# Residual products of the second block as 512 columns, an up projection one quarter ahead, and PSUM banks as fixed places

## The chip, the core and the metric

The kernel runs on one core of one Trainium2 chip, as one launch. The time is the device time of that launch in microseconds. Before the change it is 3416.86 us, the median of three runs (3407.37 to 3424.01). The profile is one further execution.

## What is computed

512 tokens of width 1024 go through two blocks of two layers each. Block 1 (norm, a mixed attention and convolution stage, an output product) is left as it is. The change is in block 2, of which each of the two layers computes:

```python
xn = rmsnorm(x, norm1_g[l])
h = xn @ w_in[l]                      # four mixers: gdn, diff, swa, mlstm
...
branch = jnp.einsum('bsnw,nwd->bsnd', ys, w_branch[l])
gate = jax.nn.sigmoid(jnp.einsum('bsd,dne->bsne', xn, w_gate[l]))
x = x + jnp.sum(gate * branch, axis=2) @ w_out[l]          # 1024 x 1024
xn = rmsnorm(x, norm2_g[l])
x = x + jnp.square(jax.nn.relu(xn @ w_mlp1[l])) @ w_mlp2[l]  # 1024 -> 4096 -> 1024
```

After the last layer a final norm is written out. All products must hold float32 accuracy.

## The kernel before

Every large product is made of three: activations and weights are each split into a high and a low part (fp32r), and high x high, high x low and low x high are summed in a PSUM bank of 128 x 512 floats. `terms(kt)` (L111) lists the 3 x kt products of a tile: first, for each k, the high weight with both activation parts, then the low weights. A token tile j is 128 of the 512 tokens.

**Weights.** `weights` (L346 on) takes 2048 columns' worth of weight per partition (8 k tiles of 256 columns, or 4 of 512), in two halves. Each half is loaded from memory by SP into `w` or `wx` (L295), copied to the high part on ACT (L367, 128 x 1024), and subtracted on POOL in four pieces of 256 columns to give the low part (L371). High and low parts have two buffers each, so a chunk can be prepared once the chunk before the last is through on PE.

**Products.** `gemm_T` (L397 on) has the weights stationary and 512 tokens moving (L405); `gemm_tile` (L408 on) has a token tile's activations stationary and weight columns moving (L413). Both open a bank with the tag `g`.

**Second block, layer by layer.** First the mixers: two chains of work, `gdn` and `others`, run side by side, the latter on banks with the tag `bS`, rope transposes and attention scores among them; `gdn` uses halves of the two `A` banks. Then gates and branches (`branch`), which sum into `mix`; `gated` splits `mix` into high and low on ACT (L1034) and DVE (L1035), chunk by chunk of 128 channels. Then w_out: `add_last` multiplies in four column blocks of 256, adds each tile to the residual x on DVE (L1012), does blocks 0 and 1 for all tiles, then blocks 2 and 3 tile by tile, each tile followed by its norm: squares on ACT (L322), a power on POOL (L301), a scaling on DVE (L329), eight transposes on PE (L334) into two banks, and the split into high and low (L337, L338).

Then the MLP in four quarters c of the 4096 hidden values. `up(c, e)` makes 256 of them: relu on ACT (L1055), square on POOL (L1056), high part on ACT (L1057), low part on DVE (L1058), into buffers `fhi` and `flo`, two of each. The down projection of a quarter is 4 column blocks x 4 tiles x 24 products, with the add L1012. The order is up(0), up(1, 0), down(0), up(1, 1 to 3), up(2, 0), down(1), and so on; the last is up(3, 1 to 3), then down(3) through `add_last` with the next layer's norm, or the final one.

**What sets the order.** The code is recorded in the order in which it is written; a scheduler then orders each engine's queue by that order and by its own idea of when operands are there. Engines run their queues in order. PSUM tiles came from pools: block 1 had two banks for each of `g`, `S`, `T`, `O`; block 2 two for `g`, three for `bS`, one for `bO` and two for `A`. Each use of a bank was a new tile, which the pool put into whichever bank of its tag was free. The pool of block 1 was closed before that of block 2 was opened.

Of the kernel before, what the change touches and what calls it, by code (L numbers as in the profile page):

```python
# [10 lines left out]
FT = mybir.dt.float32  # L11
# [7 lines left out]
T, D, L = 512, 1024, 2  # L19
NT = T // 128  # L20

PSUM_BUFS = {"g": 2, "S": 2, "T": 2, "O": 2, "bS": 3, "bO": 1}


class Arena:
# [22 lines left out]
A, AR, B0, B, C0, CR, C = Arena(), Arena(FR), Arena(), Arena(), Arena(), Arena(FR), Arena()  # L48
# [16 lines left out]
M1, M2, MR = Arena(), Arena(), Arena(FR)  # L65
# [22 lines left out]
X, G0, G, GR, P, PR = Arena(), Arena(), Arena(), Arena(FR), Arena(), Arena(FR)  # L88
# [17 lines left out]
def seg(w_ap, lo, n, kt=8):  # L106

    return w_ap[:, lo:lo + n].rearrange("(k p) n -> p k n", p=128)


def terms(kt):  # L111


    return [(0, y, k) for k in range(kt) for y in range(2)] + [(1, 0, k) for k in range(kt)]


class Consts:
# [5 lines left out]
    def add(self, name, a):  # L123
        a = np.asarray(a, np.float32)
        full = np.zeros((128, a.shape[1]), np.float32)
        full[:a.shape[0]] = a
        self.off[name] = (self.n, a.shape[1])
        self.n += a.shape[1]
        self.cols.append(full)
# [63 lines left out]
class K:  # L193
# [67 lines left out]
    def t(self, shape, tag):  # L261
        ar, tile_, turn = next(a for a in reversed(self.arenas) if tag in a[0].at)
        at, n, bufs = ar.at[tag]
        i = turn[tag] = (turn.get(tag, -1) + 1) % bufs
        m = math.prod(shape[1:])
        assert m <= n, tag
        t = tile_[:shape[0], at + i * n:at + i * n + m]
        if len(shape) == 2:
            return t
        d = " ".join("abcd"[:len(shape) - 1])  # L270
        return t.rearrange("p (%s) -> p %s" % (d, d), **{"abcd"[i]: shape[i + 1] for i in range(len(shape) - 1)})
# [2 lines left out]
        return self.t([128, n], tag)  # L274

    def bank(self, tag):
        return self.ps.tile([128, 512], FT, name="ps_" + tag, tag=tag, bufs=PSUM_BUFS[tag])

    def small_dma(self, dst, src):
        with self.nc.allow_non_contiguous_dma("small"):  # L280
# [701 lines left out]
class Block2:  # L982
# [23 lines left out]
        self.diff_lambda()  # L1006
        run((self.gdn(), 360), (self.others(box), 315))

    def add(self, n):

        x, cols = self.k.x, slice(n * 256, (n + 1) * 256)
        return lambda acc, j: self.nc.vector.tensor_add(x[:, j, cols], x[:, j, cols], acc[:, :256])  # L1012

    def add_last(self, segs, a, tiles):

        k = self.k
        for n in range(2):
            k.gemm_M(k.weights([segs[n]], 8), a, 8, 256, self.add(n))
        ws = [k.weights([segs[n]], 8) for n in (2, 3)]
        for j in range(NT):  # L1020
            for n in (2, 3):
                k.gemm_tile(ws[n - 2], a, 8, 256, j, self.add(n))
            for t in tiles:
                t(j)

    def gated(self):

        k, nc, l, ins = self.k, self.nc, self.l, self.ins
        mix = k.t([128, 8, T], "mx")
        for n in ORDER:  # L1030
            self.branch(n, mix)
        mhi, mlo = k.t([128, 8, T], "ahi"), k.t([128, 8, T], "alo")
        for c in range(8):
            nc.scalar.activation(mhi[:, c], mix[:, c], AF.Copy, scale=0.5)  # L1034
            nc.vector.scalar_tensor_tensor(mlo[:, c], mix[:, c], 0.5, mhi[:, c].bitcast(FT), op0=OP.mult, op1=OP.subtract)  # L1035
        xnT, tile_ = k.norm(ins["norm2_g_2"][l])
        self.add_last([seg(ins["w_out_2"][l], n * 256, 256) for n in range(4)], (mhi, mlo), [tile_])
        return xnT

    def mlp(self, xnT, norms):  # L1040
        k, nc, l, ins = self.k, self.nc, self.l, self.ins
        w1, w2 = ins["w_mlp1_2"][l], ins["w_mlp2_2"][l]
        hs = {}

        def up(c, e):

            if e == 0:
                hs[c] = k.t([128, 8, T], "fhi"), k.t([128, 8, T], "flo")
            w = k.weights([seg(w1, c * 1024 + e * 256, 256)], 8)
            for b in range(2):  # L1050
                def ev(acc):
                    hh, hl = hs[c]
                    m = 2 * e + b
                    r, s = k.slot("fr"), k.slot("fs")
                    nc.scalar.activation(r, acc, AF.Relu)  # L1055
                    nc.gpsimd.tensor_mul(s, r, r)  # L1056
                    nc.scalar.activation(hh[:, m], s, AF.Copy)  # L1057
                    nc.vector.tensor_sub(hl[:, m], s, hh[:, m].bitcast(FT))  # L1058
                k.gemm_T(w, xnT, 8, b * 128, ev, pieces=2 if c == e == 0 else 1)
        for c in range(4):  # L1060
            for e in range(1 if c else 0, 4):
                up(c, e)
            segs = [seg(w2[c * 1024:(c + 1) * 1024], n * 256, 256) for n in range(4)]
            if c < 3:
                up(c + 1, 0)
                for n in range(4):
                    k.gemm_M(k.weights([segs[n]], 8), hs[c], 8, 256, self.add(n))
            else:
                res, tiles = norms()
                self.add_last(segs, hs[c], tiles)  # L1070
        return res

    def others(self, d0):
# [730 lines left out]
def body(tc, ins, const_ap, cmap, out):  # L1804
    nc = tc.nc
    with ExitStack() as ctx:
        k = K(tc, ins, const_ap, cmap, ctx)
        psum = lambda n: tc.tile_pool(name="ps%d" % n, bufs=2, space=bass.MemoryType.PSUM)
        by_tile = lambda a: a.rearrange("(j p) d -> p j d", p=128)
        x_in = by_tile(ins["x"][0])  # L1810

        def to_layer(g_ap):

            res, tile_ = k.norm(g_ap)
            return res, [tile_, k.spill]

        def last():
            _, tile_ = k.norm(ins["final_norm_g_2"], out=k.x)
            return None, [tile_, lambda j: nc.sync.dma_start(by_tile(out)[:, j], k.x[:, j])]

        def between():
            _, tile_ = k.norm(ins["final_g"], out=k.x)
            res, tiles = to_layer(ins["norm1_g_2"][0])
            return res, [tile_] + tiles

        k.tp = "T"
        with k.open("A", A, AR), psum(1) as k.ps:
            blocks = [Block1(k, l) for l in range(L)]
            with k.open("C", C0, CR, C):
                x = k.x = k.t([128, NT, D], "x")  # L1830
                hT, tile_ = k.norm(ins["norm_g"][0])
                for j in range(NT):
                    k.load(x[:, j], x_in[:, j])
                    if j == 0:
                        k.load_ident()
                    if j == 1:
                        blocks[0].load_first()
                    tile_(j)
                k.load_consts()
            for l in range(L):  # L1840
                hT = blocks[l].layer(hT, None if l else x_in,
                                        (lambda: to_layer(ins["norm_g"][l + 1])) if l < L - 1 else between)
        k.tp = "bS"
        with psum(2) as k.ps:
            banks = [k.ps.tile([128, 512], FT, name="ps_A%d" % i, tag="A%d" % i, bufs=1) for i in range(2)]
            k.halves, k.turn = [b[:, z:z + 256] for z in (0, 256) for b in banks], 0
            for l in range(L):
                b = Block2(k, l)
                with k.open("M", M1, M2, MR):
                    b.mixers(hT)  # L1850
                with k.open("X", X):
                    with k.open("G", G0, G, GR):
                        xnT = b.gated()
                    with k.open("P", P, PR):
                        hT = b.mlp(xnT, (lambda: to_layer(ins["norm1_g_2"][l + 1])) if l < L - 1 else last)


# [24 lines left out]
```

## Time and profile before

| | us |
|---|---|
| median of three runs | 3416.86 |
| the profiled execution | 3411.11 |
| its span, first to last instruction | 3409.2 |
| PE busy (share of the span) | 3200.6 (94%) |
| DVE busy | 1568.6 (46%) |
| ACT busy | 1401.8 (41%) |
| POOL busy | 1400.4 (41%) |
| mean granted clock of PE | 0.987 |

The stages of the profiled execution, read from its order of time: block 1 to about 794 us; first layer of block 2: mixers to 1412, gates and branches to 1666, w_out to 1726, MLP to 2106; second layer: mixers to 2720, gates to 2973, w_out to 3034, MLP and final norm to the end. A granted clock of 1.00 is 2.4 GHz, 0.50 is 1.2 GHz. Ends of matmuls in the trace are modelled, so distances between starts say more than durations; "idle before" is the time that the engine stood still ahead of a row, with what ended it.

### The profile page before, as it was taken

Reading aid. Unit: us, or ns where it says so; the run is one execution under the profiler, and the core shown is the slowest. Engines: PE = TensorE matmul, PEld = TensorE weight load, DVE = VectorE, ACT = ScalarE, POOL = GpSimd, SP = SyncE. Lnnn points to the kernel's source line nnn. Section 1 sums busy time; section 2 is a strip of 40 time slices with the busy share of each in tenths; the row PEclk is TensorE's granted clock in tenths of the full one; section 3 lists DMA queues with packets and bytes.
Section 4 is the critical chain, followed back from the end, with each engine's and each line's share of the span. In section 5 each row is a group of like instructions: output and inputs, shape, how many; then the busy total and the mean of one; then the engine's idle time right before and its main releaser. Section 6 shows DMA issues by size and latency. Waiting matters only on the chain. (4 is left out here: it accounts for less than half of the span.)

```text
span 3409.2 us, 52506 instructions
## 1 busy us (share of the span) xinstructions
PE 3200.6 (94%) x19358; PEld 2693.2 (79%) x19358; DVE 1568.6 (46%) x3832; ACT 1401.8 (41%) x3129; POOL 1400.4 (41%) x1809
## 2 busy tenths in 40 slices
PE   7899989997899899999999999999989999999998
PEld 6576667666788778788889888788778788789998
DVE  5746584664687565322321114577675412321112
ACT  3245423543465465523332222455565532332222
POOL 5332352314411322455566554421332355555554
PEclk9999999998999999999999999999999999999999
DMA  5341324213211211433323333221121243323231
GB/s 136 91 107 44 65 78 118 63 40 89 67 30 32 73 57 38 137 112 118 99 87 93 93 99 86 72 49 32 51 68 50 87 132 110 112 80 99 87 100 68
DMA packets 334449, 277.13 MB, mean 81 GB/s; under 512 B 114024, under 2 KB 312040, under 8 KB 332784
## 3 DMA queue, kind: packets, MB, share of 16 engines
q1 hardware_dynamic: 334048, 273.38, 27.3%
q8 instruction: 152, 2.49, 0.3%
q14 instruction: 105, 0.86, 0.1%
q0 software_dynamic: 144, 0.39, 0.1%
HBM read 257.26 MB, written 16.86 MB: 80 GB/s over the span
## 5 line engine op out<-in xcount | busy, mean ns | idle before, releaser
L405 PE MATMUL ps_g<-all 128*128 128x512 f32 (+1 forms) x5184 | 1255.9, 394 | 21.0 <-DVE B L723 12.0
L405 PEld LDWEIGHTS ps_g<-all 128*128 128x128 f32 x5184 | 951.1, 190 | 209.8 <-DVE B L723 13.7
L371 POOL TENSOR_TENSOR all<-all,all 128x256 fp32r<-128x256 f32 x1024 | 784.4, 799 | 616.0 <-PE ps_g L405 197.1
L413 PE MATMUL ps_g<-all 128*128 128x256 f32 (+1 forms) x4224 | 658.6, 303 | 10.2 <-ACT all L305 2.9
L413 PEld LDWEIGHTS ps_g<-all 128*128 128x128 f32 x4224 | 565.5, 194 | 45.2 <-issue 12.3
L371 POOL TENSOR_TENSOR all<-X,all 128x256 fp32r<-128x256 f32 x448 | 328.2, 765 | 486.3 <-ACT all L367 379.7
L413 PE MATMUL ps_g<-all,P 128*128 128x256 f32 x3072 | 377.1, 285 | 15.1 <-ACT P L1057 7.8
L413 PEld LDWEIGHTS ps_g<-all,P 128*128 128x128 f32 x3072 | 374.2, 194 | 17.3 <-DVE X L1012 8.5
L367 ACT ACTIVATE all<-all 128x1024 fp32r<-128x1024 f32 x256 | 268.4, 1055 | 123.7 <-PE ps_g L405 61.0
L367 ACT ACTIVATE all<-X 128x1024 fp32r<-128x1024 f32 x112 | 118.2, 1055 | 384.1 <-PE ps_g L413 239.6
L371 POOL TENSOR_TENSOR all<-A,all 128x256 fp32r<-128x256 f32 x144 | 135.6, 973 | 305.4 <-ACT all L367 212.3
L1012 DVE TENSOR_TENSOR X<-X,ps_g 128x256 f32<-128x256 f32 x160 | 66.8, 420 | 321.3 <-PE ps_g L413 321.3
L301 POOL TENSOR_TENSOR M<-M,ct 128x2 f32<-128x2 f32 (+1 forms) x64 | 52.0, 814 | 382.2 <-DVE M L300 362.2
L1058 DVE TENSOR_TENSOR P<-P,P 128x512 fp32r<-128x512 f32 x64 | 44.3, 692 | 346.8 <-ACT P L1057 346.8
L405 PE MATMUL ps_g<-G,all 128*128 128x512 f32 x768 | 176.0, 389 | 0.4 <-DVE G L1799 0.4
L405 PEld LDWEIGHTS ps_g<-G,all 128*128 128x128 f32 x768 | 144.0, 188 | 31.1 <-DVE G L1799 1.2
L492 ACT ACTIVATE A<-A 128x128 f32<-128x128 f32 (+3 forms) x160 | 89.2, 558 | 101.0 <-DVE A L490 100.0
L1799 DVE SCALAR_TENSOR_TENSOR G<-G,ps_g 128x512 f32<-128x512 f32 x48 | 32.9, 685 | 212.3 <-PE ps_g L405 212.3
L1057 ACT ACTIVATE P<-P 128x512 fp32r<-128x512 f32 x64 | 40.4, 632 | 182.6 <-POOL P L1056 182.6
L457 PE MATMUL ps_bS<-ct,M 128*128 128x128 f32 x456 | 76.4, 283 | 37.4 <-DVE M L1678 9.0
L1301 ACT COPY M<-ps_A 128x256 f32<-128x256 f32 x224 | 81.3, 376 | 73.2 <-PE ps_A L1300 62.4
L1387 PE MATMUL ps_A<-M 128*128 128x128 f32 x640 | 101.8, 286 | 2.6 <-ACT M L1381 1.7
(379 smaller groups left out, 4265.8 us busy)
## 6 DMA issues: line engine op xcount, KB each, us to landing
all<-in_w_in_dram SPq DMA_DIRECT2D x100, 512.0 KB, 3.7
X<-in_w_mlp_dram SPq DMA_DIRECT2D x64, 512.0 KB, 3.6
all<-in_w_mlp_dram SPq DMA_DIRECT2D x64, 512.0 KB, 3.6
all<-in_w_gate_dram SPq DMA_DIRECT2D x40, 512.0 KB, 3.7
X<-in_w_gate_dram SPq DMA_DIRECT2D x24, 512.0 KB, 3.6
A<-in_w_in_dram SPq DMA_DIRECT2D x16, 512.0 KB, 3.8
all<-in_w_in_dram SPq DMA_DIRECT2D x64, 128.0 KB, 2.8
G<-yd SPq DMA_DIRECT2D x8, 1024.0 KB, 5.7
```

What stands on the lines that cost most here:

```text
L301: return nc.gpsimd.tensor_tensor(ss, ss, self.mhalf[:ss.shape[0], :n], op=OP.pow)
L367: nc.scalar.activation(hi, w, AF.Copy)
L371: nc.gpsimd.tensor_sub(lo[:, q:q + 256], w[:, q:q + 256], hi[:, q:q + 256].bitcast(FT))
L405: nc.tensor.matmul(acc[:, cols], w[x][:, k, m0:m0 + 128], a[y][:, k, cols], start=i == 0, stop=i == n - 1)
L413: nc.tensor.matmul(acc[:, :n], a[y][:, k, j * 128:(j + 1) * 128], w[x][:, k, :n], start=i == 0, stop=i == 3 * kt - 1)
L457: nc.tensor.transpose(tp[:, i * 128:i * 128 + s.shape[0]], s, self.ident[:s.shape[0], :s.shape[0]])
L492: nc.scalar.activation(p, p, AF.Exp, scale=-1.0, bias=mn, accum_out=sm)
L1012: return lambda acc, j: self.nc.vector.tensor_add(x[:, j, cols], x[:, j, cols], acc[:, :256])
L1057: nc.scalar.activation(hh[:, m], s, AF.Copy)
L1058: nc.vector.tensor_sub(hl[:, m], s, hh[:, m].bitcast(FT))
L1301: evac(dst, tp)
L1387: nc.tensor.matmul(zp[:, bs[c]], Xt[:, bs[c]], Y[d][:, bs[c]], start=True, stop=True)
```

## The change

It has three parts. First, w_out and the down projections: a column block is 512 wide, and its four token tiles have one bank each, open at the same time; the weights come as two chunks of 4 k tiles x 512 columns. All tiles take the first chunk's twelve products, then all the second's, and then the tile is added. Where norms follow, the second column block goes tile by tile, both chunks. Second, the whole next quarter of the up projection stands ahead of a down projection, where before it was its first 256 columns; so the last down projection follows another down projection. Third, eight PSUM tiles are made once, and `BANKS` gives each tag a fixed list of them in each of three phases (block 1; the mixers; the rest of block 2), which are taken in turn. From the gates on, `g` has six banks, and two serve the norms' transposes.

```diff
+BANKS = ({"g": (0, 1), "S": (2, 3), "T": (4, 5), "O": (6, 7)}, {"g": (0, 1), "bS": (2, 3, 4), "bO": (5,), "A": (6, 7)},
+         {"g": (0, 1, 6, 7, 2, 3), "bS": (4, 5)})
...
     def bank(self, tag):
-        return self.ps.tile([128, 512], FT, name="ps_" + tag, tag=tag, bufs=PSUM_BUFS[tag])
+        r = self.rings[tag]
+        r.append(r.pop(0))
+        return r[-1]
+
+    def use_banks(self, phase):
+        self.rings = {t: [self.ps[i] for i in b] for t, b in BANKS[phase].items()}
...
-    def add_last(self, segs, a, tiles):
-
-        k = self.k
+    def add_rows(self, w_ap, a, tiles=None):
...
+        k, nc, x = self.k, self.nc, self.k.x
         for n in range(2):
-            k.gemm_M(k.weights([segs[n]], 8), a, 8, 256, self.add(n))
-        ws = [k.weights([segs[n]], 8) for n in (2, 3)]
-        for j in range(NT):
-            for n in (2, 3):
-                k.gemm_tile(ws[n - 2], a, 8, 256, j, self.add(n))
-            for t in tiles:
-                t(j)
+            cols = slice(n * 512, n * 512 + 512)
+            acc = [k.bank("g") for _ in range(NT)]
+
+            def part(w, b, j):
+                for i, (u, y, kk) in enumerate(terms(4)):
+                    nc.tensor.matmul(acc[j], a[y][:, 4 * b + kk, j * 128:(j + 1) * 128], w[u][:, kk], start=b == i == 0,
+                                     stop=b == 1 and i == 11)
+                if b:
+                    nc.vector.tensor_add(x[:, j, cols], x[:, j, cols], acc[j])
+            ws = []
+            for b in range(2):
+                ws.append(k.weights([seg(w_ap[b * 512:b * 512 + 512], n * 512, 512, 4)], 4, n=512))
+                if tiles is None or n == 0:
+                    for j in range(NT):
+                        part(ws[b], b, j)
+            if tiles is not None and n == 1:
+                for j in range(NT):
+                    for b in range(2):
+                        part(ws[b], b, j)
+                    for t in tiles:
+                        t(j)
...
         for c in range(4):
-            for e in range(1 if c else 0, 4):
-                up(c, e)
-            segs = [seg(w2[c * 1024:(c + 1) * 1024], n * 256, 256) for n in range(4)]
+            for i in range(c and c + 1, min(c + 2, 4)):
+                for e in range(4):
+                    up(i, e)
+            rows = w2[c * 1024:(c + 1) * 1024]
             if c < 3:
-                up(c + 1, 0)
-                for n in range(4):
-                    k.gemm_M(k.weights([segs[n]], 8), hs[c], 8, 256, self.add(n))
+                self.add_rows(rows, hs[c])
             else:
                 res, tiles = norms()
-                self.add_last(segs, hs[c], tiles)
+                self.add_rows(rows, hs[c], tiles)
```

The order of the built programs shows where instructions stand. PE between block 1 and block 2: 512 columns are block 1's last w_out products, 128x128 from `ct` the norms' transposes, 256 columns the first products of block 2. Lines 334, 405 and 413 of before are 341, 412 and 420 now. Before:

```order
L413 MATMUL ps_g_6157<-all1_76 128x512 x11
L413 MATMUL ps_g_6171<-all1_76 128x512 x12
L334 MATMUL ps_T_6141<-ct_60,A0_82 128x128 x4
L334 MATMUL ps_T_6149<-ct_60,A0_82 128x128 x4
L334 MATMUL ps_T_6198<-ct_60,A0_82 128x128 x4
L334 MATMUL ps_T_6206<-ct_60,A0_82 128x128 x4
L413 MATMUL ps_g_6253<-all1_76 128x256 x24
```

Now:

```order
L420 MATMUL ps1_83<-all1_76 128x512 x12
L420 MATMUL ps0_82<-all1_76 128x256 x4
L341 MATMUL ps4_86<-ct_60,A0_93 128x128 x4
L420 MATMUL ps0_82<-all1_76 128x256
L341 MATMUL ps5_87<-ct_60,A0_93 128x128 x4
L420 MATMUL ps0_82<-all1_76 128x256 x19
L420 MATMUL ps1_83<-all1_76 128x256 x24
L420 MATMUL ps0_82<-all1_76 128x256 x11
L341 MATMUL ps4_86<-ct_60,A0_93 128x128 x4
L420 MATMUL ps0_82<-all1_76 128x256
L341 MATMUL ps5_87<-ct_60,A0_93 128x128 x4
L420 MATMUL ps0_82<-all1_76 128x256 x12
```

All 256-column products stood behind the last four groups of transposes; 59 of the first 96 now stand ahead of the last two groups, and one between these.

PE at the first layer's last up projection (L405, L412) and the following down projection. Before:

```order
L405 MATMUL ps_g_16472<-all1_76 128x512 x24
L405 MATMUL ps_g_16501<-all1_76 128x512 x24
L413 MATMUL ps_g_16543<-all1_76,P1_13969 128x256 x14
L413 MATMUL ps_g_16569<-all1_76,P1_13969 128x256 x2
L413 MATMUL ps_g_16543<-all1_76,P1_13969 128x256
L413 MATMUL ps_g_16569<-all1_76,P1_13969 128x256 x5
L413 MATMUL ps_g_16543<-all1_76,P1_13969 128x256 x9
```

Now:

```order
L412 MATMUL ps2_84<-all1_76 128x512 x24
L412 MATMUL ps3_85<-all1_76 128x512 x24
L1027 MATMUL ps0_82<-all1_76,P1_12949 128x512 x12
L1027 MATMUL ps1_83<-all1_76,P1_12949 128x512 x12
L1027 MATMUL ps6_88<-all1_76,P1_12949 128x512 x12
L1027 MATMUL ps7_89<-all1_76,P1_12949 128x512 x12
```

Before, this is down(3) on the quarter just made, in pieces of two tiles in turn; now it is down(2), with twelve products to each of four banks, and down(3) comes 192 products later. The names of the hidden values (`P1`) don't tell the quarters apart.

PE at the norm behind w_out of the first layer, first tile. Before:

```order
L413 MATMUL ps_g_13693<-all1_76 128x256 x24
L413 MATMUL ps_g_13740<-all1_76 128x256 x21
L334 MATMUL ps_bS_13725<-ct_60,X0_11748 128x128 x4
L413 MATMUL ps_g_13740<-all1_76 128x256 x2
L334 MATMUL ps_bS_13733<-ct_60,X0_11748 128x128 x4
L413 MATMUL ps_g_13740<-all1_76 128x256
```

Now:

```order
L1027 MATMUL ps6_88<-all1_76 128x512 x24
L1027 MATMUL ps7_89<-all1_76 128x512 x13
L341 MATMUL ps4_86<-ct_60,X0_11016 128x128 x4
L1027 MATMUL ps7_89<-all1_76 128x512
L341 MATMUL ps5_87<-ct_60,X0_11016 128x128 x4
L1027 MATMUL ps7_89<-all1_76 128x512 x10
```

The transposes of tile 0 stood behind 21 narrow products of tile 1, and 2 lay between their two groups; now it is 13 wide ones, and one.

The queue of POOL keeps its order but for the squares L1056 of 30 up tiles, which move with their up projection. ACT, DVE and PE have other orders in places of the mixers too; numbers and shapes of the instructions there are the same.

## Rows read from the trace of the kernel before

**Rows 1.** Stretches: us, busy (count) of PE, PEld, DVE, ACT, POOL; clock, DMA, GB/s.
```profile
794.00:1412.00 618.00, 578.79 (x3889) 498.74 (x3890) 390.35 (x1047) 330.22 (x907) 180.92 (x230) 0.98 0.21 56
...
1412.00:1666.00 254.00, 251.61 (x1110) 206.79 (x1110) 63.20 (x91) 81.14 (x116) 134.58 (x181) 1.00 0.39 127
...
1726.00:2106.00 380.00, 367.03 (x2385) 337.11 (x2385) 62.37 (x123) 112.12 (x152) 218.40 (x297) 0.99 0.30 94
```

**Rows 2.** Order of time, PE, MLP: start, us, line, tiles, count [idle before].
```profile
1786.01 40.58 PE L413 MATMUL ps_g<-all,P 128*128 128x256 f32 x336 [1.21 <-DVE X L1012]
...
1826.43 43.71 PE L405 MATMUL ps_g<-all 128*128 128x512 f32 x192
...
1869.98 5.91 PE L413 MATMUL ps_g<-all,P 128*128 128x256 f32 x48
```

**Rows 3.** Waits of PE, whole span: total us, times, longest.
```profile
PE ps_bS L457 <- DVE M L1678: 9.0, 8, 2.6
...
PE ps_bS L457 <- DVE M L1592: 8.4, 14, 1.4
...
PE ps_g L413 <- ACT P L1057: 7.8, 2, 3.9
...
PE ps_g L413 <- DVE X L1012: 7.2, 6, 1.2
...
PE ps_g L413 <- DVE all L1035: 2.0, 4, 0.8
...
PE ps_g L413 <- ACT all L1034: 1.4, 2, 0.7
...
PE ps_g L405 <- ACT G L1774: 1.3, 1, 1.3
```

**Rows 4.** PE in order of time, block 1's w_out; its add (ns min/median/max).
```profile
762.44 5.48 PE L413 MATMUL ps_g<-all 128*128 128x512 f32 x23
...
L610 DVE TENSOR_TENSOR C<-C,ps_g x32: 674/686/689, 306.8 to 781.0; 128x512 f32<-128x512 f32 x32
```

**Rows 5.** Order of time, POOL and DVE, before the first down projection.
```profile
1783.20 1.04 POOL L1056 TENSOR_TENSOR P<-P 128x512 f32<-128x512 f32 x1
...
1784.93 0.69 DVE L1058 TENSOR_TENSOR P<-P,P 128x512 fp32r<-128x512 f32 x1 [7.92 <-ACT P L1057]
...
1785.54 0.74 DVE L1012 TENSOR_TENSOR X<-X,ps_g 128x256 f32<-128x256 f32 x2
```

**Rows 6.** Stretches, as rows 1, behind the last down projection's wait.
```profile
2045.00:2050.00 5.00, 2.74 (x13) 2.74 (x14) 0.69 (x1) 0.63 (x1) 1.54 (x2) 0.56 0.48 160
...
2050.00:2055.00 5.00, 5.00 (x35) 5.00 (x35) 0.84 (x2) 0.00 (x0) 0.00 (x0) 0.76 0.00 0
```

**Rows 7.** Order of time, POOL and DVE, last weight chunk of w_out.
```profile
1691.60 2.83 POOL L371 TENSOR_TENSOR all<-X,all 128x256 fp32r<-128x256 f32 x4 [5.91 <-PE ps_g L413]
...
1692.21 0.42 DVE L1012 TENSOR_TENSOR X<-X,ps_g 128x256 f32<-128x256 f32 x1 [2.46 <-PE ps_g L413]
...
1694.39 2.83 POOL L371 TENSOR_TENSOR all<-all,all 128x256 fp32r<-128x256 f32 x4
```

**Rows 8.** Order of time, PE and DVE, start of w_out.
```profile
1665.76 2.03 PE L413 MATMUL ps_g<-all 128*128 128x256 f32 x13
...
1671.05 1.13 DVE L1035 SCALAR_TENSOR_TENSOR all<-G,all 128x512 fp32r<-128x512 f32 x1 [0.69 <-ACT all L1034]
```

**Rows 9.** Order of time, PE, between the blocks (two answers).
```profile
780.54 1.94 PE L334 MATMUL ps_T<-ct,A 128*128 128x128 f32 x8 [4.92 <-DVE A L329]
...
790.23 2.22 PE L334 MATMUL ps_T<-ct,A 128*128 128x128 f32 x8 [7.75 <-DVE A L329]
...
793.86 14.33 PE L413 MATMUL ps_g<-all 128*128 128x256 f32 x96 [1.41 <-DVE all L338]
...
808.02 0.82 PE L457 MATMUL ps_bS<-ct,M 128*128 128x128 f32 x6
```

**Rows 10.** Stretch, as rows 1, between the blocks.
```profile
795.00:800.00 5.00, 5.00 (x27) 5.00 (x26) 0.62 (x3) 0.00 (x0) 2.31 (x5) 0.53 0.77 166
```

**Rows 11.** Order of time, PE, transposes of the norm behind w_out.
```profile
1708.49 0.66 PE L334 MATMUL ps_bS<-ct,X 128*128 128x128 f32 x4 [0.62 <-DVE X L329]
```

More of the change, by code (lines that the diff above doesn't have):

```diff
@@ L20 @@
 NT = T // 128
-PSUM_BUFS = {"g": 2, "S": 2, "T": 2, "O": 2, "bS": 3, "bO": 1}
+BANKS = ({"g": (0, 1), "S": (2, 3), "T": (4, 5), "O": (6, 7)}, {"g": (0, 1), "bS": (2, 3, 4), "bO": (5,), "A": (6, 7)},
+         {"g": (0, 1, 6, 7, 2, 3), "bS": (4, 5)})
 class Arena:
@@ L1007, in mixers @@
         run((self.gdn(), 360), (self.others(box), 315))
-    def add(self, n):
-        x, cols = self.k.x, slice(n * 256, (n + 1) * 256)
-        return lambda acc, j: self.nc.vector.tensor_add(x[:, j, cols], x[:, j, cols], acc[:, :256])
-    def add_last(self, segs, a, tiles):
-        k = self.k
-        for n in range(2):
-            k.gemm_M(k.weights([segs[n]], 8), a, 8, 256, self.add(n))
-        ws = [k.weights([segs[n]], 8) for n in (2, 3)]
-        for j in range(NT):
-            for n in (2, 3):
-                k.gemm_tile(ws[n - 2], a, 8, 256, j, self.add(n))
-            for t in tiles:
-                t(j)
+    def add_rows(self, w_ap, a, tiles=None):
+        k, nc, x = self.k, self.nc, self.k.x
+        for n in range(2):
+            cols = slice(n * 512, n * 512 + 512)
[18 more added lines that the diff above has]
+                        t(j)
     def gated(self):
@@ L1036, in gated @@
         xnT, tile_ = k.norm(ins["norm2_g_2"][l])
-        self.add_last([seg(ins["w_out_2"][l], n * 256, 256) for n in range(4)], (mhi, mlo), [tile_])
+        self.add_rows(ins["w_out_2"][l], (mhi, mlo), [tile_])
         return xnT
@@ L1807, in body @@
         k = K(tc, ins, const_ap, cmap, ctx)
-        psum = lambda n: tc.tile_pool(name="ps%d" % n, bufs=2, space=bass.MemoryType.PSUM)
+        ps = ctx.enter_context(tc.tile_pool(name="ps", bufs=1, space=bass.MemoryType.PSUM))
+        k.ps = [ps.tile([128, 512], FT, name="ps%d" % i, tag="ps%d" % i) for i in range(8)]
         by_tile = lambda a: a.rearrange("(j p) d -> p j d", p=128)
@@ L1826, in body @@
         k.tp = "T"
-        with k.open("A", A, AR), psum(1) as k.ps:
+        k.use_banks(0)
+        with k.open("A", A, AR):
             blocks = [Block1(k, l) for l in range(L)]
@@ L1843, in body @@
         k.tp = "bS"
[L1844 to L1855, printed above, removed]
+        for l in range(L):
+            b = Block2(k, l)
+            k.use_banks(1)
+            k.halves, k.turn = [b_[:, z:z + 256] for z in (0, 256) for b_ in k.rings["A"]], 0
+            with k.open("M", M1, M2, MR):
+                b.mixers(hT)
+            k.use_banks(2)
+            with k.open("X", X):
+                with k.open("G", G0, G, GR):
+                    xnT = b.gated()
+                with k.open("P", P, PR):
+                    hT = b.mlp(xnT, (lambda: to_layer(ins["norm1_g_2"][l + 1])) if l < L - 1 else last)
 _INS = [
```

## Prediction

> **What bounds the kernel now.** First busy time by stage [rows 1]: in the first layer's mixers of the second block (794 to 1412 us) PE is busy 578.8 of 618 us with DVE at 390; in its gates and branches (1412 to 1666) 251.6 of 254; in its MLP (1726 to 2106) 367.0 of 380, with DVE 62, ACT 112, POOL 218. So the MLP, where most of the change lies, is a PE stage: it gets shorter only by what PE no longer issues or no longer waits for. Second, PE's order of time in the MLP [rows 2], from start to start so that modelled ends don't matter: 336 products of 256 columns take 1826.43 - 1786.01 = 40.42 us, 120.3 ns each; the next 192 of 512 columns take 1869.98 - 1826.43 = 43.55 us, 226.8 ns each. Two narrow products cost 240.6 ns, one wide one 226.8: 13.8 ns belong to a product whatever its width. Third, PE's waits [rows 3], which say where it stands still.
>
> **Wide products.** In each layer w_out had 384 narrow products and the down projection 1536, together 3840 in two layers; now there are 1920 wide ones. PE is full there, so the whole difference is on the path: 1920 x 13.8 ns = **26.5 us less**. The wide price stems from up products, whose stationary operand is the weight. Block 1's w_out has the very form that the change takes over (activations stationary, 512 weight columns, twelve to a run): 23 of them span 5.48 us [rows 4], or about 227 ns each with the last one's tail of 0.5 us taken off. Against this stands a rule of the Trainium skill, "TensorE: Matmul & The Clock Gate", section "Back-to-back issue gap": a warm product takes N/2.4 + 2.5 ns. It would give 109.2 and 215.8 ns, both some 11 below the rows, and 2.5 ns per pair; the gain by it would be an estimated 4.8 us in place of 26.5. The rows were measured on these very products, so I take theirs.
>
> **Waits on the two g banks.** At the first down tiles of c = 0, 1, 2 PE waits 1.2 us for the residual add, six times, 7.2 us [rows 3]. The chain is in [rows 5]: the last up tile's square (L1056) stands on POOL behind eight weight subtractions and starts at 1783.20; the subtraction of the low half on DVE, which depends on it, ends at 1785.6; behind that in DVE's queue stand the first two adds. With six banks, and the first add only after five runs of twelve (13.6 us of PE), nothing waits: **7.2 us less**.
>
> **Up projection a quarter ahead.** The last down projection followed the last up directly, and its first tile waited 3.9 us for the hidden values, in both layers 7.8 us [rows 3]. Behind that idle time the granted clock reads 0.56 and 0.76 [rows 6], partly the lower level of 1.2 GHz: 2.74 and 5.00 us of work hold 13 and 35 products, where 120.3 ns each make it 5.8 us. So each such wait costs 2.0 us more. In the new order down(2), some 43 us of PE work, stands between: **7.8 + 4.0 = 11.8 us less**. What is late next? The eight up chunks that now open the MLP ask POOL for eight subtractions, two times 2.83 us [rows 7], and two squares of 1.04 [rows 5], 7.7 us per 10.9 us of PE, as the up chunks of before did without a PE wait; POOL keeps its cover. hs has two buffers; up(c+1) writes the one that down(c-1) has left, which stands ahead of it on PE.
>
> **Head of w_out.** The first narrow products run through all eight k and wait for the last chunks of mix on ACT and DVE: 2.0 + 1.4 us [rows 3]. The first 48 wide products (10.9 us) use k 0 to 3 only, and the last chunk was ready 6.4 us after the stage's start [rows 8]. An evacuation wait of 1.3 us in the gates, ended by ACT L1774 [rows 3], goes with the six banks: together **4.7 us less**.
>
> **From block 1 to block 2.** Here one set of pools closed and another opened, and none of the second block's products stood ahead of the last transposes of block 1's norms. PE idles 4.92 and 7.75 us, then 1.41 [rows 9]; the granted clock is 0.53 still in 795 to 800 [rows 10], so the first 96 products take 808.02 - 793.86 = 14.16 us against 96 x 120.3 ns = 11.55. With fixed banks 60 of these 96 stand ahead of the last transposes. Worked through: the first idle time stays but for 4 products. From 782.5 on PE has 54 in a row, which begin at the lower level, some 6 us as after 793.86, and end near 791.4. The last transposes, ready at 790.2, follow until 793; the remaining 36 products need the last tile's halves (some 0.5 us later than the 793.9 of before, with DVE's rope steps of the first tiles ahead of them) and end near 797.5. That is 10.5 us earlier than 808.0; I take **10 us less**, between 0 (the next weights bind) and 14.1 (all of the idle time).
>
> **Norm tiles.** At the end of w_out and of each MLP a tile's transposes stood behind 21 narrow products of the next one (2.53 us), and PE waited 0.6 us and more [rows 11]; they now stand behind 13 wide ones (2.95 us). The add ahead of the norm grows from 0.42 [rows 7] to 0.69 us [rows 4], so the chain is 0.26 longer and its cover 0.42: about 0.16 x 12 = **2 us less**. The four last tiles have no such cover and pay the 0.26: **1 us more**.
>
> **Weights of the last wide chunk.** Their low half waits for its buffer. Before, POOL began 2.4 us after the chunk's last tile did (which ended at 1692.1 and took 24 x 120.3 ns), as soon as PE had done 20 of its 24 products, and took 2 x 2.83 us [rows 7]. Now 10 of 12 wide products (2.27 us) precede it; it ends 5.2 us after PE leaves the chunk, and PE needs the last piece 2.72 + 11 x 0.227 = 5.2 after. **1 us more** for four such places, between 0 and 8 (POOL slowed).
>
> **Mixers and block 1.** All counts stay; the scheduler's order moves in the mixers, hardly in block 1. The pool gave an opening whichever bS bank came free; in the built program of before 30 of 336 openings take one out of turn. Now each of these waits for its turn, while the other stream fills in. No row shows such a wait. The nearest, waits on bS for data, average 8.4/14 = 0.6 and 9.0/8 = 1.1 us, the longest 2.6 [rows 3]; hidden ones cost 0, and a better order could give back half of these 17.4 us. From -9 to +78; I take 0.13 each, **4 us more**, nearer to the hidden ones, since PE has other work ready nearly everywhere there (94% busy).
>
> **Sum.** 26.5 + 7.2 + 11.8 + 4.7 + 10 + 2 - 1 - 1 - 4 = 56.2 us. The profiled execution took 3411.11 us (span 3409.2 and 1.9 around it): 3354.9. The median of the three runs lies 5.75 above it, and I carry that over: **3361 us**, 1.6% under 3416.86.
>
> **Rivals.** (a) Turn-taking in bS costs the mixers. For: three banks serve two chains, and a rope transpose holds one for long. Against: the attention steps stand at about the same places in the new order. Without the mixers' term the time is 3357 + 30p: at p = 1.1 us 3390; from p = 1.43 no measurable gain; from p = 2.57 slower, at the longest row's 2.6 **3435 us**. (b) The 13.8 ns are not saved, because runs of twelve change banks more often than the up products do: 3361 + 26.5 = 3388; block 1's row speaks against. By the Trainium skill's formula it would be an estimated 3383. (c) The new order serves the mixers: half of the 17.4 us comes back, 3348. (d) The clock. The rows show it low only behind idle time; if PE stood still more often among four open banks, a wide product at the lower level would cost up to 227 ns more, and 328 of the 1920 would eat 74 us: 3435, slower. The wide products in the gates, on two banks, had a granted 1.00 throughout [rows 1]. The Trainium skill, "TensorE: Matmul & The Clock Gate", section "A second HAM failure mode: psum-queue depth-cycling", tells of a kernel with 512 columns whose clock swings in this way; this trace does not bear it out. (e) The boundary's new order brings nothing, because the next weights bind: 3371, inside the forecast.
>
> **How the numbers follow.** Within 0.5% (17 us) of 3416.86 a measurement can't tell from no change. Forecast with (e), 3340 to 3376: 0.66. (c) 0.08. (a) at about 3390: 0.13; with p between 1.43 and 2.57: 0.04; beyond: 0.02. (b) 0.05. (d) 0.02. Faster 0.66 + 0.08 + 0.13 + 0.05 = 0.92, same 0.04, slower 0.04. The range runs from 3340, the forecast's low end, to 3395, just above (b) and (a) at 1.1.
>
> **What would show it.** PE's order of time in the MLP: wide products 227 ns apart, nothing idle between up and down, no clock below 1.00 before the norms. The waits for L1012 and L1057 gone; at 775 to 797 products among the transposes. Wrong would be: PE waiting for the new add or for POOL's weights, mixers of 618 us that grow by over 10, or products of the new line near 240 ns.

## The result, and the profile after

The changed kernel takes 3356.86 us (median of four runs, 3349.41 to 3361.52) where the kernel before, beside it, takes 3414.43: a ratio of 0.9821, 95% interval 0.9804 to 0.9838. 3361 us was predicted, with 3340 to 3395 as the range. The profiled execution of the changed kernel took 3361.52 us, span 3359.8, the slowest of the four. Lines have moved: L413 is L420 now, or L1027 for the new products; L405 is L412, L334 L341, L457 L464, L371 L378; the add L1012 is L1030.

PE's order of time in the first layer's MLP, answering to [rows 2]:

```profile
1803.31 43.68 PE L1027 MATMUL ps<-all,P 128*128 128x512 f32 x192
1846.83 43.68 PE L412 MATMUL ps<-all 128*128 128x512 f32 x192
1890.35 43.68 PE L1027 MATMUL ps<-all,P 128*128 128x512 f32 x192
1933.87 43.68 PE L412 MATMUL ps<-all 128*128 128x512 f32 x192
1977.39 70.66 PE L1027 MATMUL ps<-all,P 128*128 128x512 f32 x311
2048.36 3.47 PE L1027 MATMUL ps<-all,P 128*128 128x512 f32 x14 [0.31 <-POOL all L378]
```

From start to start 192 products take 43.52 us, 226.7 ns each, down and up alike. Nothing idles between them; the one bracket is the new wait for the low half of the last weights. Head of w_out:

```profile
1663.21 27.13 PE L1027 MATMUL ps<-all 128*128 128x512 f32 x119
1690.65 3.47 PE L1027 MATMUL ps<-all 128*128 128x512 f32 x14 [0.31 <-POOL all L378]
```

The first 119 products run through, where [rows 3] had waits for L1034 and L1035. The stretches of the first layer's mixers and of its MLP, with the columns of [rows 1]:

```profile
797.56:1420.79 623.23, 576.79 (x3834) 495.32 (x3832) 388.89 (x1045) 335.72 (x927) 180.13 (x232) 0.98 0.21 59
...
1740.00:2070.00 330.00, 327.67 (x1455) 270.22 (x1454) 51.65 (x78) 100.36 (x135) 195.70 (x266) 1.00 0.30 96
```

The MLP's clock is 1.00. The mixers, whose work has not changed, are longer. PE's waits over the whole span (total us, times, longest), answering to [rows 3]:

```profile
PE ps L464 <- DVE M L1695: 18.2, 16, 3.0
...
PE ps L1289 <- issue: 6.5, 2, 3.3
...
PE ps L420 <- DVE M L952: 4.1, 2, 2.1
...
PE ps L1027 <- POOL all L378: 1.2, 4, 0.3
```

The waits for L1012, L1057, L1034, L1035 and L1774 have no row any more. The first three rows here all lie in the mixers. The first of them isn't twice the 9.0 us that [rows 3] has for the same step (L1678 before). In the kernel before, a second step of that chain had a row beside it, and that step, L1682 now, has none any more:

```profile
PE ps_bS L457 <- DVE M L1665: 7.5, 6, 2.0
```

Together the two come to 16.5 us before and 18.2 after. Between the blocks, answering to [rows 9]:

```profile
781.77 1.12 PE L341 MATMUL ps<-ct,A 128*128 128x128 f32 x4 [3.91 <-DVE A L336]
...
783.61 7.12 PE L420 MATMUL ps<-all 128*128 128x256 f32 x54
791.62 0.66 PE L341 MATMUL ps<-ct,A 128*128 128x128 f32 x4 [0.90 <-DVE A L336]
...
793.17 4.55 PE L420 MATMUL ps<-all 128*128 128x256 f32 x36
797.56 0.82 PE L464 MATMUL ps<-ct,M 128*128 128x128 f32 x6
...
806.47 3.13 PE L420 MATMUL ps<-all 128*128 128x256 f32 x24 [2.08 <-DVE M L952]
811.60 3.62 PE L420 MATMUL ps<-all 128*128 128x256 f32 x16 [2.00 <-DVE M L952]
```

54 products fill the former idle time of 7.75 us, and the block's first rope transposes (L464) start 15.8 us after 781.77, where they started 27.5 us after the like point of before. Then, 9 and 14 us later, come two new waits of 2 us.

The stages of two profiles of either kernel (the second from the runs r4_before and r1_after below), cut at the same instructions, in us:

| stage | before | after | gain (means) | predicted |
|---|---|---|---|---|
| between the blocks, third pair of last transposes to first rope | 27.5, 27.6 | 15.8, 15.8 | 11.7 | 10 |
| mixers, layer 1 | 614.8, 617.9 | 623.2, 620.1 | -5.3 | |
| mixers, layer 2 | 612.7, 615.8 | 619.7, 620.4 | -5.8 | -4 for both |
| gates and branches, both layers | 487.5, 487.3 | 484.8, 484.9 | 2.6 | 1.3 |
| w_out, MLP and norms, both layers | 886.2, 886.8 | 834.5, 834.4 | 52.1 | 48.9 |
| sum | | | 55.3 | 56.2 |

All stages but the mixers repeat within 1 us.

### The profile page after: what moved, and what is told of

It reads as the page before. It is cut to its first block, busy times and chain, and to the rows that moved or that the text cites. A ratio compares the mean times of both kernels' runs of the same rounds, so it can differ in the third digit from the quotient of the medians.

```text
span 3359.8 us, 48319 instructions
## 1 busy us (share of the span) xinstructions
PE 3177.3 (95%) x17438; PEld 2595.8 (77%) x17438; DVE 1550.2 (46%) x3752; ACT 1400.9 (42%) x3129; POOL 1396.7 (42%) x1809
## 3 DMA queue, kind: packets, MB, share of 16 engines
q1 hardware_dynamic: 313568, 273.38, 27.6%
## 5 line engine op out<-in xcount | busy, mean ns | idle before, releaser
L412 PE MATMUL ps<-all 128*128 128x512 f32 (+1 forms) x5184 | 1256.0, 394 | 18.6 <-DVE B L730 12.0
L412 PEld LDWEIGHTS ps<-all 128*128 128x128 f32 x5184 | 951.6, 190 | 207.5 <-DVE B L730 13.7
L378 POOL TENSOR_TENSOR all<-all,all 128x256 fp32r<-128x256 f32 x1024 | 782.7, 799 | 652.5 <-ACT all L374 247.3
L420 PE MATMUL ps<-all 128*128 128x256 f32 (+1 forms) x3456 | 574.1, 311 | 9.3 <-DVE M L952 4.1
L420 PEld LDWEIGHTS ps<-all 128*128 128x128 f32 x3456 | 480.2, 198 | 42.3 <-issue 12.5
L378 POOL TENSOR_TENSOR all<-X,all 128x256 fp32r<-128x256 f32 x448 | 328.0, 765 | 436.8 <-ACT all L374 334.0
L1027 PE MATMUL ps<-all,P 128*128 128x512 f32 x1536 | 351.3, 390 | 0.6 <-POOL all L378 0.6
L1027 PEld LDWEIGHTS ps<-all,P 128*128 128x128 f32 x1536 | 288.0, 188 | 60.9 <-POOL all L378 1.5
L374 ACT ACTIVATE all<-all 128x1024 fp32r<-128x1024 f32 x256 | 268.1, 1054 | 102.5 <-PE ps L412 50.5
L374 ACT ACTIVATE all<-X 128x1024 fp32r<-128x1024 f32 x112 | 118.2, 1055 | 347.7 <-PE ps L1027 152.1
L378 POOL TENSOR_TENSOR all<-A,all 128x256 fp32r<-128x256 f32 x144 | 135.2, 971 | 304.5 <-ACT all L374 188.1
L1076 DVE TENSOR_TENSOR P<-P,P 128x512 fp32r<-128x512 f32 x64 | 44.3, 692 | 332.9 <-ACT P L1075 332.9
L1030 DVE TENSOR_TENSOR X<-X,ps 128x512 f32<-128x512 f32 x80 | 55.0, 687 | 292.0 <-PE ps L1027 292.0
L412 PE MATMUL ps<-G,all 128*128 128x512 f32 x768 | 175.4, 389 | 0.0
L412 PEld LDWEIGHTS ps<-G,all 128*128 128x128 f32 x768 | 144.2, 188 | 29.9
L464 PE MATMUL ps<-ct,M 128*128 128x128 f32 x456 | 79.3, 285 | 37.9 <-DVE M L1695 18.2
L1318 ACT COPY M<-ps 128x256 f32<-128x256 f32 x224 | 81.0, 375 | 80.8 <-PE ps L1317 69.5
L1404 PE MATMUL ps<-M 128*128 128x128 f32 x640 | 103.3, 286 | 2.7 <-ACT M L1398 2.2
```

Of the source, the lines that this page charges most:

```text
L374: nc.scalar.activation(hi, w, AF.Copy)
L378: nc.gpsimd.tensor_sub(lo[:, q:q + 256], w[:, q:q + 256], hi[:, q:q + 256].bitcast(FT))
L412: nc.tensor.matmul(acc[:, cols], w[x][:, k, m0:m0 + 128], a[y][:, k, cols], start=i == 0, stop=i == n - 1)
L420: nc.tensor.matmul(acc[:, :n], a[y][:, k, j * 128:(j + 1) * 128], w[x][:, k, :n], start=i == 0, stop=i == 3 * kt - 1)
L464: nc.tensor.transpose(tp[:, i * 128:i * 128 + s.shape[0]], s, self.ident[:s.shape[0], :s.shape[0]])
L1027: nc.tensor.matmul(acc[j], a[y][:, 4 * b + kk, j * 128:(j + 1) * 128], w[u][:, kk], start=b == i == 0, stop=b == 1 and i == 11)
```

## The experiments

What was open was the mixers, and which part of the change brings what. **Theory A**: the mixers pay because bS banks are taken strictly in turn, the prediction's mechanism. **Theory B**: with fixed tiles the scheduler put the mixers' work into another order, and that order costs, whichever bank is used. **Theory C**: much of the loss is the scatter of single executions. Ratios are to runs of the kernel before on the same chip, with 95% intervals.

**e1_pool_turns: the pool's turns on fixed tiles.** The list holds the bS banks as the pool of before gave them.

```diff
     def bank(self, tag):
+        if tag == "bS" and self.order:
+            return self.ps[int(self.order.pop(0))]
         r = self.rings[tag]
```

> The changed kernel, but in the mixers the three bS banks are handed out in the very sequence in which the pool of the kernel before gave them (156 openings per layer, 15 of them out of turn), as a written list; the queues of DVE and ACT keep the order of the changed kernel. Theory A (taking bS banks in turn costs the mixers): they get back what they lost, 8.4 and 7.0 us in the profile of the changed kernel, about 3342 us. Theory B (what costs is the order in which the scheduler put the mixers' work, whichever bank is given): 3357 us, within 4, and mixers of 623 and 620 us. Theory C (the mixers' loss is the clock in that one execution): 3357 us too, with mixers that differ from the 623 and 620 us by several us in either direction.

3360.11 us, 0.9842 (0.9827 to 0.9856); mixers 620.8 and 618.4 us, and both odd waits unchanged (L1703 and L1297 are L1695 and L1289 of the changed kernel):

```profile
PE ps L472 <- DVE M L1703: 18.2, 16, 3.0
...
PE ps L1297 <- issue: 6.5, 2, 3.3
```

So A falls: the same turns as before give none of these waits back.

**e5_before_pools and e6_g_pool: wide products and early up on pools.** In e5 the pools are those of the kernel before; in e6 (second diff) `k.pg`, a pool for g alone, is open throughout the program.

```diff
-            acc = [k.bank("g") for _ in range(NT)]
+            acc = [k.bank("g"), k.bank("g"), k.A[0], k.A[1]]
```

```diff
+        ps = self.pg if tag == "g" else self.ps
```

> Wide products and the up projection a quarter ahead, on the pools of the kernel before; the four open banks are the two g banks and the two A banks, which nobody uses outside the mixers. The mixers' DVE and ACT queues stand in the order of the kernel before. Theories A and B: mixers at 615 and 613 us again (15 less than in the changed kernel), the boundary between the blocks as before (10 more, less the 4 that the first mixers gave back) and the wait for L1774 back: 3357 - 15 + 6 + 1 = 3349 us. Theory C: the mixers gain nothing, 3357 + 11 = 3368 us.

> As the run with the pools of the kernel before, but the two g banks in a pool of their own that is open for the whole program. PE's queue between the blocks then reads as in the changed kernel (60 of the first 96 products ahead of the last transposes), the mixers' DVE and ACT queues as in the kernel before. Theories A and B: boundary 10 us earlier, mixers 615 and 613 us but for what the first one gives back: 3340 to 3345 us, better than the changed kernel. Theory C: 3358 us.

e5: 3361.45 us, 0.9848 (0.9833 to 0.9863), mixers 615.5 and 614.4, between the blocks 27.6. e6: 3352.10 us, 0.9820 (0.9806 to 0.9834), mixers 616.8 and 614.4, between the blocks 15.8. The waits of 3 us at L1289 are in neither. So the whole gain between the blocks comes from g's being open across the border; nothing else need be fixed for it. And in both MLPs 370 and 354 us are reached with two g and two A banks: it is four open banks, not fixed places, that end the waits for the add. Both times lie above what B promised, by 12 and by 7 to 12 us: the mixers are shorter by what it says, the whole is not. Two to three microseconds of that lie in w_out, MLP and norms, which take 837.2 us in e5 and 836.5 in e6 against 834.4 in the changed kernel.

**e8_bS_fixed: e6 with fixed tiles for bS and bO alone.**

```diff
+        if tag in ("bS", "bO"):
+            r = self.rings[tag]
+            r.append(r.pop(0))
+            return r[-1]
```

> As the run with the g pool of its own, but bS and bO get fixed tiles that are taken in turn, as in the changed kernel; g stays in its pool, the open banks stay two g and two A. In the built program DVE and ACT then have the changed kernel's order in the mixers. Theory B (that order costs): the mixers of 616.8 and 614.4 us become 621 to 625 and 618 to 620 us, with waits of 3.1 and 3.3 us ahead of the transposes L1289 of the changed kernel that end on nothing shown; about 3352 + 11 = 3363 us. Rival (the run with the g pool won by its banks for g or by chance): mixers under 618 us, 3352 us.

3354.81 us, 0.9835 (0.9817 to 0.9852). The wait is there, and has a name now (L1279 here is L1281 of the changed kernel), but the mixers took 615.0 and 614.7 us:

```profile
PE ps_bS L462 <- DVE M L1693: 17.5, 16, 3.0
...
PE ps_A L1287 <- DVE M L1279: 6.0, 2, 3.0
```

That contradicts B as a full account, so the same programs were run again.

**r1_after, r2_g_pool, r3_bS_fixed, r4_before: the same again.** No edit; r2 is e7 below.

> The changed kernel once more, for a second profile and for times beside the next two runs. Theory B (its order of the mixers' work costs): mixers of 619 to 624 us again in both layers, 3357 us. Theory C (a good part of the 15 us is that one execution): mixers nearer to 617 us, waits of PE in the mixers still some 2 us a layer above those of the orders made with pools.

> The kernel with the g pool and the two A banks first, once more: the order of the kernel before in the mixers. Theory B: mixers of 612 to 618 us, and 8 to 12 us faster than the changed kernel beside it. Theory C: mixers of 612 to 618 us too, but only 2 to 5 us faster than the changed kernel beside it.

> The kernel with the g pool and fixed bS and bO tiles once more; on every engine its mixers stand in the changed kernel's order, and yet its first profile showed mixers of 615 us. Theory B falls if they stay there: then the order alone doesn't cost, and what differs from the changed kernel is which banks are which. Theory C: between 614 and 621 us, as it happens, with PE's waits in the mixers 39 to 44 us a layer.

> The kernel before once more, for a second profile: mixers of 615 and 613 us within 2 us, PE's waits in them at 40 us a layer, if these are of the order; block 1, which no run here changes, shows by how much a stage differs between executions.

r1: 3361.83 us, 0.9832 (0.9817 to 0.9847). r2: 3358.40, 0.9825 (0.9804 to 0.9846). r3: 3366.82, 0.9846 (0.9830 to 0.9863). r4: 3416.43, 0.9997 (0.9986 to 1.0008). So r2 is 3.4 us faster than r1 beside it, as C said and not the 8 to 12 of B. r4's mixers took 617.9 and 615.8 us, 3 longer than in the first profile of the same kernel, where 2 had been allowed. The stretches of the two mixers, first of e8, then of r3, one and the same program:

```profile
795.20:1410.15 614.95, 572.70 (x3833) 491.86 (x3832) 389.61 (x1045) 335.73 (x927) 180.40 (x232) 0.98 0.22 60
2080.16:2694.87 614.71, 574.44 (x3834) 492.16 (x3832) 391.02 (x1046) 335.06 (x927) 178.53 (x228) 0.98 0.21 59
```

```profile
798.93:1419.51 620.58, 576.75 (x3833) 495.35 (x3832) 388.91 (x1045) 335.62 (x927) 180.57 (x232) 0.98 0.21 59
2088.88:2710.98 622.10, 578.32 (x3833) 496.10 (x3832) 392.63 (x1047) 335.95 (x928) 178.57 (x228) 0.97 0.21 58
```

5.6 and 7.4 us lie between two executions of one program. All profiles together, grouped by the order in which the mixers stand in the built program, means of seven each, in us:

| order of the mixers | layer 1 (lowest to highest) | layer 2 | PE's waits in them |
|---|---|---|---|
| as before: before, r4, e4, e5, e6, e7, r2 | 616.0 (614.2 to 617.9) | 615.2 (612.5 to 620.4) | 40.8 and 40.4 |
| as after: e2, after, r1, e1, e3, e8, r3 | 620.3 (615.0 to 625.3) | 619.3 (614.7 to 622.1) | 44.1 and 42.3 |

The new order costs some 4 us a layer, 8.4 in all; by the scatter of the seven profiles that is known to somewhat over 4 us (95%). 5.2 us of it are waits; most of the rest is PE's busy time, which differs by 8 us between e8 and r3, one and the same program. So B accounts for about half of the 15.4 us that the first pair of profiles showed (by that interval for a quarter to five sixths), and C for the rest.

One place where the order bites is seen at 859 us. PE, then DVE, of the changed kernel:

```profile
852.33 3.03 PE L420 MATMUL ps<-all 128*128 128x256 f32 x24
855.20 1.09 PE L1672 MATMUL ps<-M 128*128 128x512 f32 x4
859.42 0.93 PE L1289 MATMUL ps<-ct,M 128*128 128x128 f32 x4 [3.13 <-issue]
```

```profile
857.77 0.94 DVE L1681 TENSOR_SCALAR M<-M 128x512 f32<-128x512 f32 x1
858.63 0.68 DVE L1281 SCALAR_TENSOR_TENSOR M<-M 128x512 f32<-128x512 f32 x1
```

The four transposes of `gdn` need the result of L1281, which ends at 859.31 and stands in DVE's queue behind a scaling of the other chain (L1681). The same place in the kernel before:

```profile
859.05 3.04 PE L413 MATMUL ps_g<-all 128*128 128x256 f32 x24
861.93 0.60 PE L1272 MATMUL ps_A<-ct,M 128*128 128x128 f32 x4
```

Here 24 products of the other chain stand directly ahead of the same transposes, and nothing waits. "Issue" in the first fence was thus a wait for DVE that the profile had not named; e8 names it. It stands in all seven profiles of the new order, twice, and in none of the old one. It doesn't explain the loss alone: e8 has it too (6.0 us), and yet PE's waits in e8's mixers sum to 80.4 us, no more than the 81.2 of the old order. Which other places cost or give back stays open.

**e7_g_pool_A_first: e6 with the A banks first.**

```diff
-            acc = [k.bank("g"), k.bank("g"), k.A[0], k.A[1]]
+            acc = [k.A[0], k.A[1], k.bank("g"), k.bank("g")]
```

> As the run with the g pool of its own, but of the four open banks the two A banks come first, so that w_out's first tiles don't have to wait until the last gate's evacuation leaves the g banks. Theory: w_out is 1.1 and 1.5 us shorter in the two layers (the waits for the gates' evacuation, L1810 of that run, of 0.5 us each gone), nothing else moves: 3352 - 2.6 = 3349.5 us. Rival: the up products behind a down projection now wait for the adds of the g banks, up to 0.7 us at each of eight places: 3352 + 3 = 3355 us.

3356.63 us, 0.9835 (0.9822 to 0.9848). In the profile w_out falls from 56.4 to 55.5 us in both layers, 1.7 us of the 2.6 expected, and no wait for an add appears; in the time this drowns. Neither e6 nor e7 can be told from the changed kernel.

**e2_places_only: fixed places on the kernel before.** The diff's part on `BANKS`, `bank` and `use_banks`, and nothing of `add_rows` and `mlp`.

> The kernel before with the fixed PSUM places alone: narrow products, up projection as before. All theories: between the blocks about 10 us earlier at the 96th product, the waits for L1012 (7.2 us) and for L1774 (1.3 us) gone. Theories A and B: the mixers lose some 15 us in all, so that 3 us are won, 3411 us, no difference that can be measured. Theory C: the mixers stay at 615 and 613 us, 3396 us.

3403.31 us, 0.9964 (0.9950 to 0.9977): between the two expected times. Its profile shows 11.7 us less between the blocks, 8.0 less in the MLPs, 2.6 less in the gates, 1 more in w_out and mixers of 625.3 and 619.3 us, the longest of the group.

**e4_ahead_only and e3_late_up: the up projection.** e4 is the kernel before with only the new order of `up`; e3 is the changed kernel with the old one.

```diff
-            for i in range(c and c + 1, min(c + 2, 4)):
-                for e in range(4):
-                    up(i, e)
+            for e in range(1 if c else 0, 4):
+                up(c, e)
```

> The kernel before with the up projection a quarter ahead, nothing else: narrow products, pools. Theory: the two waits of 3.9 us for L1057 go, and the clock behind them: 3415 - 11.8 = 3403 us. Rival (the clock is not won): 3407 us. Both: the waits for the add L1012 stay at about 7 us, since two g banks still feed the first down tiles; the mixers, whose order is untouched, stay at 615 and 613 us.

> The changed kernel with the old order of the up projection: up(c + 1, 0) alone ahead of down(c). Theory: the last down projection of each layer waits 3.9 us for its hidden values (L1064 of this kernel) and finds the clock low behind that wait, 2.0 us more: 3357 + 11.8 = 3369 us. Rival: only the wait itself comes back, 3357 + 7.8 = 3365 us. Both: no new wait at the other down projections, since six banks are free for them, and wide products 227 ns apart as before.

e4: 3404.02 us, 0.9971 (0.9958 to 0.9983). Its MLPs take 384.2 and 368.3 us instead of 390.6 and 374.0, some 12 less where the waits themselves were 7.8. The granted clock reads 1.00 in it from 2030 to 2070 us, where down(3) follows, so the clock behind the wait was won with it; the waits for the add stay at 7.2 us. e3: 3356.92 us, 0.9835 (0.9818 to 0.9853), as fast as the changed kernel. PE of e3, from the last up of the quarter to the last down projection:

```profile
1983.76 32.80 PE L412 MATMUL ps<-all 128*128 128x512 f32 x144
2016.40 27.14 PE L1027 MATMUL ps<-all,P 128*128 128x512 f32 x119
```

No bracket stands at 2016.40, though this down projection follows its own up projection at once. Its MLPs take 369.1 and 354.3 us, those of the changed kernel 369.5 and 354.3. Both theories of this run were wrong: beside the new products the early up projection brings nothing.

e2 and e3 differ by the wide products alone (`add_rows` in place of `add` and `add_last`), and so show what these bring. w_out, MLP and norms of both layers take 879.5 us in e2 and 834.3 in e3, 45.1 less; in e2's waits the 7.8 us for the hidden values still stand, and in e3's they don't.

## Why the prediction was right, step by step

**Wide products**: right. 226.7 ns in the MLP against 226.8 forecast, 26.7 us in place of 26.5; rival (b) is out. The formula of the Trainium skill, "TensorE: Matmul & The Clock Gate", section "Back-to-back issue gap", gives 215.8 ns for such a product. The section says that it is meant for an isolated product, which the prediction left out, and that a stream of products with 512 columns takes about 131 ns each. This trace agrees with neither figure: its stream is 11 ns above the first on average. The same page's section "A second HAM failure mode: psum-queue depth-cycling" was rival (d)'s company: with four open banks the granted clock of the MLP reads 1.00, so it didn't happen in that stretch.

**Waits for the add and the head of w_out**: right. The waits are gone, and e2's MLPs are 8.0 us shorter where 7.2 was forecast. e5 adds that four open banks suffice.

**Up a quarter ahead**: right in size (some 12 against 11.8 us, e4), wrong in taking the early up projection to be needed for it. "In the new order down(2), some 43 us of PE work, stands between" is true, but isn't needed. The wide products go by rows: the first 48 of them use k 0 to 3 only, the hidden values of the first two up chunks, and last 10.9 us. In e3 the low half of the quarter's last hidden values (L1076 there) is ready at 2023.11, 6.7 us after the down projection's start:

```profile
2022.42 0.69 DVE L1076 TENSOR_TENSOR P<-P,P 128x512 fp32r<-128x512 f32 x1 [7.81 <-ACT P L1075]
```

That is the prediction's own argument at the head of w_out; it was not carried over to the down projection. Since the gain was counted once, the sum stayed right.

**From block 1 to block 2**: 11.7 us against 10, and the pieces as worked out: 54 products in a row, the last transposes at 791.6, the remaining 36 behind them. What was missed came after. ACT, then DVE, of the changed kernel:

```profile
801.13 1.06 ACT L374 ACTIVATE all<-all 128x1024 fp32r<-128x1024 f32 x1 [2.32 <-PE ps L420]
802.10 1.06 ACT L538 ACTIVATE M<-ps 64x512 fp32r<-64x512 f32 x2
```

```profile
802.70 2.04 DVE L539 SCALAR_TENSOR_TENSOR M<-ps,M 64x512 fp32r<-64x512 f32 x3 [3.72 <-DMA M<-in_gdn_conv_w_dram]
...
810.67 0.15 DVE L1226 TENSOR_SCALAR M<-M 128x1 f32<-128x1 f32 x1 [3.86 <-DMA M<-in_gdn_norm_g_dram]
```

The first ropes now reach ACT while it copies weights (L374), so that L538 and behind it DVE's L539 start late; the second idle time of DVE ends with the load of a small constant. Behind each, PE waits 2 us for the rope steps L952: up to 4 us are given back within the mixers (2 in e6, where one of the two waits is left). The DMA named at L539 is doubtful, since L539 also needs L538; in r2 the same idle time, 3.49 us, is put down to that step on ACT.

Which waits appear there isn't fixed by the program: r2 has one of 1.9 us, and e7, the same program, has two others of 2.5 and about 0.6 us, as have e1 and e3. In these three a rope step on DVE (L954 of the changed kernel), which takes 0.28 us where POOL is idle, takes 2.93 to 2.95 us. It starts within 0.02 us of POOL's weight subtractions. DVE, then POOL, of e1:

```profile
801.66 2.93 DVE L962 TENSOR_TENSOR M<-M 128x128 f32<-128x128 f32 x1
```

```profile
801.66 5.82 POOL L386 TENSOR_TENSOR all<-all,all 128x256 fp32r<-128x256 f32 x8
```

In the changed kernel's own profile the step ran at 798.50, beside a memset of POOL and before its next subtractions at 799.27, and took 0.28 us.

**Norm tiles**: right in direction, 1 us net forecast, and 2.0 less in the waits for the scaling. Before, then after:

```profile
PE ps_bS L334 <- DVE X L329: 13.9, 18, 2.7
```

```profile
PE ps L341 <- DVE X L336: 11.9, 18, 2.7
```

**Last weights**: right, four waits of 0.3 us, 1.2 in all.

**Mixers and block 1**: the mis-sized term. "I take 0.13 each, 4 us more" was built on turns in bS, and e1 shows that the turns are not what costs. What costs is the order, some 8 us (about half of what the first pair of profiles showed), and the one place shown, at L1289, writes an A bank, of which no row on bS could have told. The bounds, -9 to +78, held it. The prediction had seen that "the scheduler's order moves in the mixers" and weighed only the banks. In the sum the 4 us too little were made good by w_out, MLP and gates, 4.5 us better than forecast. Of these 1.3 are in the gates: the wait for L1774 had one row of 1.3, but the second layer's gates fell by 2.

**The time itself**: that 3361 lies so near 3356.86 is in part luck. The prediction added 5.75 us, since its profiled execution lay below the median; the profiled execution of the changed kernel is the slowest of four, 4.7 above. Profile to profile 49.6 us were gained, median to median 57.6, and the forecast of 56.2 was worked out from a profile.

## What to carry to other kernels

Cost a part of a change on top of the others, not alone: two parts here removed the same wait, and one of them could have been left out. Changing how buffers are handed out changes what a scheduler makes of code that nobody touched, so compare the built order there, and look for a step that has lost the work that stood ahead of it. And profile the same program twice before a loss of 1% in a stage is explained.

## What the runs showed of the hardware

One program's mixers took 615.0 and 614.7 us in one execution, 620.6 and 622.1 in another, with the same products; PE's busy time in them went from 1147 to 1155 us and the waits from 80.4 to 85.4. For the whole program the time goes with the mean granted clock only loosely: the eight runs of r4 range from 3411.38 us at 0.986 to 3423.88 at 0.981, but the four at 0.984 alone lie from 3411.77 to 3421.14, and r1's run at 0.986 (3361.83) is slower than two of its runs at 0.984. Block 1, whose work no kernel here changes, reaches the same transposes between 778.8 and 787.0 us. What makes an execution longer or shorter, and what sets its clock, stays open.

A DVE step of 0.28 us that reads and writes SBUF alone took 2.93 to 2.95 us in three executions in which it started together with POOL's subtractions. Without work on POOL beside it the same line took at most 0.29 us (38 times in e1).
